# First stage of a streaming encoder on one core: small vectors by GpSimd's queue, the second tile's x loaded behind the second conditions, the first tile two quarters ahead, and throwaway products

## The chip, the core and the metric

The kernel runs on one core of one Trainium2 chip. A core has a matrix engine (TensorE, PE in the profile; PEld is its loading of the stationary operand), a vector engine (VectorE, DVE), an activation engine (ScalarE, ACT), GpSimd (POOL) and SyncE (SP), each with its own queue of instructions that it runs in order. DMA transfers are issued from the queues of SP, ACT or POOL (SPq, ACTq, POOLq) and run beside the engines. The metric is the device time of one execution in microseconds, the median of several runs.

## The reference

One inference step of a two-layer encoder on 1024 prompt rows and 32 sample rows of width 1024. The first layer's mixer, with which this case is concerned, is:

```python
mod = jax.nn.silu(c) @ w_ada[i] + b_ada[i]
sh1, sc1, gt1, sh2, sc2, gt2 = jnp.split(mod[:, None, :], N_MOD, axis=-1)
h = rmsnorm(x, g_norm[i, 0]) * (1 + sc1) + sh1
z = jax.nn.gelu(h @ w_in)
u, v = jnp.split(z, 2, axis=-1)
v = rmsnorm(v, g_v)
s = jnp.einsum('gij,bnjgd->bnigd', w, vr) + b_s      # per chunk of 128 rows
mix = (u * s) @ w_out
x = x + gt1 * rmsnorm(mix, g_norm[i, 1])
```

A channel MLP (1024 to 4096 to 1024, squared ReLU) follows; the second layer has a pooling mixer in place of the gating one. All is float32.

## The kernel before

The 1056 rows are three column tiles: 384, 384 and 256 + 32. x is kept transposed, features on partitions, as eight blocks of 128 (kb 0 to 7). Every weight is split into a high part `wh` (an activation copy rounded to the matrix engine's reduced float32, L422) and a low part `wl` (a subtraction on VectorE), every activation likewise into `hh` and `hl`, and a product is the sum of three: `wh*hh`, `wh*hl`, `wl*hh`.

All loads of x, conditioning weights (w_ada) and layer weights stand in one list, `stream`. `issue()` issues them in the list's order from SP (one load of x from ACT), as far as buffers are free: the first sixteen pieces of w_ada have buffers of their own, layer weights share three raw buffers. `stream_to(kind, key)` emits the work on the list up to a piece. Every hardware-issued DMA takes one of eight semaphores in turn and waits until the transfer that had it before has landed.

The first stage is written out by hand, in a block in which each engine keeps the order of the text (`tc.manual_schedule()`, from `load_vectors(2, slice(0, 2))` on). Its steps, by the names that the profile shows:

- `load_vectors`: the conditions c, then g_norm, b_ada, pool_scale and sgu_g_v, as rows (tile `row`). `turn_conditions`: silu, then a transpose (`csilT`). `turn_vectors`: transposes of the rows (`rowT`).
- `x_squares` (ACT, `xsq`): the sum of squares of a block of 128 rows of x. `x_turn`: eight PE transposes (`xT`), with two copies to `acc`, both on VectorE in tile 0, one on VectorE and one on ACT in tile 1.
- `first_norm(t)`, a generator for tile t, with the pieces `spread` (`ms_h`, `r_h`, then `pb_h` on PE and a copy by ACT), "statistics", and then `apply`: for two feature blocks at a time a scaling `mt` (VectorE), `hh` (ACT) and `hl` (VectorE). `h0`, `h1`, `h2` are the three generators, `next(h0)` emits the next piece.
- Conditioning: `do_ada_pe` multiplies silu(c) with two pieces of w_ada (`ada`, PE) and transposes the result on VectorE (`adas`). A fold, popped from `pe_folds` in the order made, gathers it on PE (`adat`) and writes scale coefficients (`coef`) or shifts (`shift`) on VectorE. `conditions(q)` does both groups (scale and shift) of quarter q, that is of feature blocks 2q and 2q + 1, and pops the first fold.
- `early_mm(bs, q)`: the first quarter-width piece of v (512 of its columns), for the row blocks bs and the feature quarter q: per block four products with `wh` (hh, hl by turns) and two with `wl`, all of 128x512 (`pv`, L973). Blocks 0 to 2 are tile 0 (called front below), 3 and 4 are tile 1 (rear); block 5 and tile 2 follow behind the stage. `early_ps` are the five PSUM banks in which they add up. Five blocks, four quarters and six products make the 120 early products.

The order of the text: conditions, x of blocks 0 and 1, vectors, x of block 2, conditions 0, statistics of tile 0; then for each quarter q: `apply` of tile 0, the products of blocks 0 to 2, (at q = 0 all of tile 1's x and statistics), `apply` of tile 1, conditions(q + 1) with a fold, the products of block 3, the other fold, the products of block 4.

What follows, from `stream_to("x", 8)` on, is tile 2's x, block 5's products and the rest of v; it is the same text in both kernels. Behind it a planner that counts PE and VectorE time weaves loading, conditioning and residual work between the products; its counts do not depend on the order inside the first stage. `sgu_group(g)` loads the spatial weights (`wt`, SP) and biases (`bs`, ACT) of a gating group, with two buffers each; the first two groups' loads have nothing to wait for and are issued during the first stage.

## Time and profile before

| | us |
|---|---|
| median of 3 runs | 2172.68 (2172.6 to 2174.59) |
| the profiled execution | 2173.74, span 2171.7 |
| PE busy | 2145.5 (99% of the span) |
| DVE, ACT, POOL busy | 1431.8, 971.3, 13.3 |
| first early product starts | 19.77 |
| x of tile 2 starts to be transposed | 68.20 |

How to read the profile: times count from the first instruction. A stretch row gives its bounds, its length, then for PE, PEld, DVE, ACT and POOL the busy time and the number of instructions, then the granted clock of TensorE (1.00 is full speed; before the first change that was recorded, at 15.89, the column shows 1.00 whatever it was), the busy share of the DMA engines and the GB/s moved. A timeline row gives start and duration, engine (with q: its queue issuing a DMA), line, operation, out<-in, shapes, the number of instructions merged, and in brackets the engine's idle time before it and what ended it. A row of the chain of waits is start, duration and what the chain ran through. Matmul ends are modelled: a matmul's row has a tail of about 0.39 us that overlaps the next.

### The profile page before, as it was taken

The numbers are of one execution on the slowest core, as the hardware profiler recorded it, in microseconds if no ns is written. First come the engines' busy times: TensorE is split into PE (matmuls) and PEld (weight loads), VectorE is DVE, ScalarE is ACT, GpSimd is POOL, SyncE is SP. The second block draws the span as 40 slices with busy tenths as digits, with TensorE's granted clock in tenths as the row PEclk, the third lists the DMA queues.
The fourth block names the chain that finished last, engine by engine and source line by source line (L and its number), as shares of the span: only waits on it lengthen the run. The fifth ranks groups of instructions, "written<-read, shape, count | busy, mean of one in ns | idle before, by whom it ended". The sixth has DMA issues, their size and how long they took to land.

```text
span 2171.7 us, 33210 instructions
## 1 busy us (share of the span) xinstructions
PE 2145.5 (99%) x13214; PEld 2078.1 (96%) x13214; DVE 1431.8 (66%) x2499; ACT 971.3 (45%) x1643; POOL 13.3 (1%) x30
## 2 busy tenths in 40 slices
PE   7999999999999999999999999999999999999998
PEld 5778899999999999999999999999999999999997
DVE  5688647566879548496747879869675554523377
ACT  4633422234447552323445566666555542313354
POOL 0000000000000000000000000000000000000001
PEclk9999999999999999999999999999999999999999
DMA  8386534343437454243645466565455552302255
GB/s 300 119 269 193 173 93 139 90 148 109 147 96 233 132 155 143 87 140 110 196 129 161 141 189 182 171 191 158 141 161 158 157 155 68 98 20 78 69 139 125
DMA packets 383262, 312.95 MB, mean 144 GB/s; under 512 B 39458, under 2 KB 346346, under 8 KB 383108
## 3 DMA queue, kind: packets, MB, share of 16 engines
q1 hardware_dynamic: 380452, 308.64, 46.8%
q8 instruction: 103, 1.69, 0.3%
q10 hardware_dynamic: 2144, 1.41, 0.2%
q0 software_dynamic: 512, 0.79, 0.1%
q14 instruction: 51, 0.42, 0.1%
HBM read 278.95 MB, written 31.84 MB: 143 GB/s over the span
## 4 chain that ended last, share of the span: by engine, by line
PE 93%; DVE 3%; DMA 2%; ACT 1%; issue 1%; ACTq 0%; DVEq 0%; SPq 0%
PE pg L902 11%; PE pg L903 11%; PE pg L904 11%; PE pf L902 11%; PE pf L904 11%; PE pf L903 11%; PE po L902 3%; PE po L903 3%; PE po L904 3%; PE pu L902 3%; PE pu L904 3%; PE pu L903 3%; PE pv L929 2%; PE pv L930 2%; PE pv L931 2%; PE pp L1532 1%
## 5 line engine op out<-in xcount | busy, mean ns | idle before, releaser
L902 PE MATMUL pg<-fh,wh_dn 128*128 128x384 f32 (+1 forms) x1536 | 495.8, 323 | 0.0
L902 PE MATMUL pf<-hh,wh_up 128*128 128x384 f32 (+1 forms) x1536 | 494.4, 322 | 0.0
L903 PE MATMUL pf<-hl,wh_up 128*128 128x384 f32 (+1 forms) x1536 | 493.1, 321 | 0.0
L904 PE MATMUL pf<-hh,wl_up 128*128 128x384 f32 (+1 forms) x1536 | 492.9, 321 | 0.2 <-DVE wl_up L79 0.2
L903 PE MATMUL pg<-fl,wh_dn 128*128 128x384 f32 (+1 forms) x1536 | 492.6, 321 | 0.4 <-DVE fl L79 0.4
L904 PE MATMUL pg<-fh,wl_dn 128*128 128x384 f32 (+1 forms) x1536 | 492.5, 321 | 0.0
L79 DVE TENSOR_TENSOR wl_up<-raw,wh_up 128x1024 fp32r<-128x1024 f32 x152 | 185.9, 1224 | 165.4 <-ACT wh_up L422 165.4
L902 PEld LDWEIGHTS pg<-fh,wh_dn 128*128 128x128 f32 x1536 | 288.3, 188 | 1.5 <-ACT fh L1121 0.6
L903 PEld LDWEIGHTS pg<-fl,wh_dn 128*128 128x128 f32 x1536 | 288.3, 188 | 1.5 <-DVE fl L79 0.7
L904 PEld LDWEIGHTS pf<-hh,wl_up 128*128 128x128 f32 x1536 | 288.6, 188 | 0.5 <-DVE wl_up L79 0.5
L903 PEld LDWEIGHTS pf<-hl,wh_up 128*128 128x128 f32 x1536 | 288.3, 188 | 0.4
L902 PEld LDWEIGHTS pf<-hh,wh_up 128*128 128x128 f32 x1536 | 288.2, 188 | 0.4
L904 PEld LDWEIGHTS pg<-fh,wl_dn 128*128 128x128 f32 x1536 | 288.3, 188 | 0.0
L422 ACT ACTIVATE wh_up<-raw 128x1024 fp32r<-128x1024 f32 x152 | 161.2, 1060 | 279.9 <-PE pf L903 213.6
L79 DVE TENSOR_TENSOR acc<-acc,pg 128x384 f32<-128x384 f32 (+1 forms) x336 | 174.2, 519 | 146.3 <-PE pg L904 145.7
L422 ACT ACTIVATE wh_dn<-raw 128x1024 fp32r<-128x1024 f32 x152 | 160.8, 1059 | 202.9 <-PE pg L903 170.6
L79 DVE TENSOR_TENSOR wl_dn<-raw,wh_dn 128x1024 fp32r<-128x1024 f32 x152 | 186.0, 1224 | 82.4 <-ACT wh_dn L422 82.2
L79 DVE SCALAR_TENSOR_TENSOR aa<-raw,csil,aa 128x512 f32<-128x512 f32 (+1 forms) x364 | 203.5, 623 | 8.0 <-DMA raw<-in_w_ada_dram 7.9
L1295 ACT ACTIVATE r<-pf 128x384 f32<-128x384 f32 (+1 forms) x192 | 86.6, 451 | 201.9 <-PE pf L904 199.2
L79 DVE TENSOR_TENSOR fl<-r,fh 128x384 fp32r<-128x384 f32 (+1 forms) x192 | 100.3, 523 | 85.4 <-ACT fh L1121 84.3
L902 PE MATMUL pu<-hh,wh_u 128*128 128x384 f32 (+1 forms) x384 | 125.8, 328 | 0.0
L902 PE MATMUL po<-ush,wh_o 128*128 128x384 f32 (+1 forms) x384 | 123.5, 322 | 0.0
(263 smaller groups left out, 2927.2 us busy)
## 6 DMA issues: line engine op xcount, KB each, us to landing
raw<-in_ffn_w_up_dram SPq DMA_DIRECT2D x152, 512.0 KB, 3.9
raw<-in_ffn_w_down_dram SPq DMA_DIRECT2D x152, 512.0 KB, 3.5
raw<-in_w_ada_dram SPq DMA_DIRECT2D x96, 512.0 KB, 4.3
raw<-in_sgu_w_in_dram SPq DMA_DIRECT2D x40, 512.0 KB, 4.4
xd<-acc SPq DMA_DIRECT2D x8, 1536.0 KB, 7.8
raw<-in_sgu_w_out_dram SPq DMA_DIRECT2D x24, 512.0 KB, 4.0
xo_r<-xd SPq DMA_DIRECT2D x32, 384.0 KB, 3.4
vd<-vt SPq DMA_DIRECT2D x32, 256.0 KB, 4.5
```

Of the source, the lines that this page charges most:

```text
L79: return op(out, *args, **kw)
L422: act(out=wh, in_=r, func=AF.Copy)
L902: mm(ps[:, :n], wh, rh, start=i == 0, stop=False)
L903: mm(ps[:, :n], wh, rl, start=False, stop=False)
L904: mm(ps[:, :n], wl, rh, start=False, stop=i == last)
L929: mm(ps[:m, :], a_h, wh[:, o : o + 512], start=k == 0, stop=False)
L930: mm(ps[:m, :], a_h, wl[:, o : o + 512], start=False, stop=False)
L931: mm(ps[:m, :], a_l, wh[:, o : o + 512], start=False, stop=k == KB - 1)
L1295: act(out=r[:, :n], in_=ps[:, :n], func=AF.Relu)
L1532: mm(ps[:, :n], wg[:, k, e * P : (e + 1) * P], A(t, 2 * g + k), start=k == 0, stop=k == 1)
```

## The change

- The four small vector loads (g_norm, b_ada, pool_scale, sgu_g_v) go by GpSimd's queue; only the conditions stay on ACT's. x of block 2 is loaded from SP.
- In the list of loads, x of tile 1 (blocks 3 to 5) stands behind the second conditions and the second quarter of v, not behind the first.
- `early_mm` takes one half of a quarter: with `wh`, or with `wl` (`second`); the `wl` subtraction of every quarter is emitted late, by `late_lo`.
- `warm(n)` multiplies a tile of ones with itself, 128x512, into the bank of block 4, which the first true product of that block clears: 10 such products at the start, 2 behind x of block 1, 6 ahead of the first quarter.
- x's squares of tile 1 are emitted beside its transposes (`x_sums`) and not when the load is reached.
- The stage's order: front quarters 0 and 1 (with tile 1's x between and behind), statistics of tile 1, rear quarters 0 and 1, then front and rear of quarters 2 and 3. Folds stand by themselves (`fold()`).
- The gating groups' `wt` and `bs` are both issued by SP, and not ahead of the load of v's piece 2, quarter 3, in the second stage.

```diff
@@ -177,10 +177,10 @@
     vec_rows = [t_m(f"row{i}") for i in range(3)]
-    def load_vectors(i, part):
+    def load_vectors(queue, i, part):
         at = sum(k for _, k in rows[i][: part.start])
         for ap, k in rows[i][part]:
-            nc.scalar.dma_start(vec_rows[i][at : at + k, :P], ap)
+            queue.dma_start(vec_rows[i][at : at + k, :P], ap)
             at += k
 
     csil = small.tile([P, KB, NV], F32, name="csil")
@@ -342,7 +342,7 @@
         for j in (8 + 2 * q, 9 + 2 * q, 2 * q, 2 * q + 1):
             add_ada(0, j)
         add_w(*v_item(0, q))
-        if q == 0:
+        if q == 1:
             for b in range(3, 6):
                 add_x(b)
     first_ada = len(stream)
@@ -407,7 +407,7 @@
                 r = work.tile([P, 1024], F32, tag="W", bufs=W_SLOTS, name=f"raw{k}")
             if kind == "x":
                 nr = P if key < 8 else DEC
-                i = (nc.scalar if key == 2 else nc.sync).dma_start(
+                i = nc.sync.dma_start(
                     r[:nr], ap.rearrange("t (k n) -> t k n", n=P)
                 )
             else:
@@ -421,7 +421,7 @@
         wl = work.tile([P, 1024], F32R, tag="W", bufs=W_SLOTS, name="wl_" + "_".join(map(str, key)))
         act(out=wh, in_=r, func=AF.Copy)
         witem[key] = (wh, wl)
-        if key == ("v", 0, 0):
+        if key[:2] == ("v", 0):
             late_lo.append(lambda: tt(out=wl, in0=r, in1=wh.bitcast(F32), op=ALU.subtract))
         else:
             tt(out=wl, in0=r, in1=wh.bitcast(F32), op=ALU.subtract)
@@ -589,13 +589,18 @@
 
 
     x_turns = deque()
+    x_sums = deque()
 
     def do_x(b, r):
-        x_squares(b, r)
         if b < 3:
+            x_squares(b, r)
             x_turn(b, r)
+            return
+        if b >= 6:
+            x_squares(b, r)
         else:
-            x_turns.append(lambda: x_turn(b, r))
+            x_sums.append(lambda: x_squares(b, r))
+        x_turns.append(lambda: x_turn(b, r))
 
     def stream_ready():
         k = state["next"]
@@ -958,25 +963,31 @@
     early_ps = [(ps_dn if b < 3 else ps_up)(f"pv0_{b}") for b in range(5)]
     h0, h1, h2 = (first_norm(t) for t in range(NT))
 
-    def early_mm(bs, q):
+    def early_mm(bs, q, second):
 
         wh, wl = witem[("v", 0, q)]
-        for second in (False, True):
-            for b in bs:
-                t, c0 = b // 3, b % 3 * P
-                tick(0.46 if second else 0.92)
-                for k in range(2):
-                    kb = 2 * q + k
-                    a_h, a_l = hh[t][:, kb, c0 : c0 + P], hl[t][:, kb, c0 : c0 + P]
-                    w = slice(k * 512, k * 512 + 512)
-                    for a in (a_h,) if second else (a_h, a_l):
-                        mm(
-                            early_ps[b],
-                            a,
-                            (wl if second else wh)[:, w],
-                            start=kb == 0 and a is a_h and not second,
-                            stop=kb == KB - 1 and second,
-                        )
+        for b in bs:
+            t, c0 = b // 3, b % 3 * P
+            tick(0.46 if second else 0.92)
+            for k in range(2):
+                kb = 2 * q + k
+                a_h, a_l = hh[t][:, kb, c0 : c0 + P], hl[t][:, kb, c0 : c0 + P]
+                w = slice(k * 512, k * 512 + 512)
+                for a in (a_h,) if second else (a_h, a_l):
+                    mm(
+                        early_ps[b],
+                        a,
+                        (wl if second else wh)[:, w],
+                        start=kb == 0 and a is a_h and not second,
+                        stop=kb == KB - 1 and second,
+                    )
+
+    fresh = onesr.unsqueeze(1).broadcast_to([P, 4, P])
+
+    def warm(n):
+
+        for _ in range(n):
+            mm(early_ps[4].rearrange("p (a b) -> p a b", a=4), onesr, fresh, start=True, stop=True)
 
     def early_end(bs):
         for b in bs:
@@ -986,47 +997,83 @@
 
         stream_to("ada", (0, 4 + q, 1))
         stream_to("ada", (0, q, 1))
+
+    def fold():
         pe_folds.pop(0)()
 
+    front, rear = (0, 1, 2), (3, 4)
+
+    def turn_x():
+        x_turns.popleft()()
+        x_sums.popleft()()
+
     with tc.manual_schedule():
-        load_vectors(2, slice(0, 2))
+        load_vectors(nc.scalar, 2, slice(0, 2))
         issue()
-        load_vectors(2, slice(2, 4))
-        load_vectors(0, slice(0, 1))
-        load_vectors(1, slice(0, 1))
+        load_vectors(nc.gpsimd, 0, slice(0, 1))
+        load_vectors(nc.gpsimd, 1, slice(0, 1))
+        load_vectors(nc.gpsimd, 2, slice(2, 4))
+        warm(10)
         turn_conditions()
         stream_to("x", 1)
+        warm(2)
+        stream_to("x", 2)
         turn_vectors()
-        stream_to("x", 2)
         next(h0)
-        conditions(0)
+        stream_to("ada", (0, 4, 1))
         statistics(h0)
+        stream_to("ada", (0, 0, 1))
+        fold()
         stream_to("w", ("v", 0, 0))
-        pe_folds.pop(0)()
-        for q in range(4):
-            next(h0)
-            if q == 0:
-                late_lo.pop()()
-            early_mm((0, 1, 2), q)
-            if q == 0:
-                stream_to("x", 5)
-                next(h1)
-                x_turns.popleft()()
-                x_turns.popleft()()
-                next(h1)
-                x_turns.popleft()()
-                statistics(h1)
-            next(h1)
-            if q < 3:
-                conditions(q + 1)
-                stream_to("w", ("v", 0, q + 1))
-                early_mm((3,), q)
-                pe_folds.pop(0)()
-                early_mm((4,), q)
-                if q == 2:
-                    stream_to("x", 6)
-            else:
-                early_mm((3, 4), q)
+        fold()
+        warm(6)
+        next(h0)
+        late_lo.pop()()
+        early_mm(front, 0, False)
+        early_mm(front, 0, True)
+        conditions(1)
+        fold()
+        stream_to("x", 5)
+        x_turns.popleft()()
+        fold()
+        next(h0)
+        x_sums.popleft()()
+        early_mm(front, 1, False)
+        late_lo.pop()()
+        turn_x()
+        early_mm(front, 1, True)
+        turn_x()
+        next(h1)
+        conditions(2)
+        statistics(h1)
+        fold()
+        next(h1)
+        early_mm(rear, 0, False)
+        early_mm(rear, 0, True)
+        fold()
+        next(h1)
+        early_mm(rear, 1, False)
+        early_mm(rear, 1, True)
+        stream_to("w", ("v", 0, 2))
+        next(h0)
+        early_mm(front, 2, False)
+        late_lo.pop()()
+        conditions(3)
+        early_mm(front, 2, True)
+        fold()
+        next(h1)
+        early_mm(rear, 2, False)
+        fold()
+        early_mm(rear, 2, True)
+        stream_to("w", ("v", 0, 3))
+        next(h0)
+        early_mm(front, 3, False)
+        late_lo.pop()()
+        next(h1)
+        stream_to("x", 6)
+        early_mm(rear, 3, False)
+        early_mm(front, 3, True)
+        early_mm(rear, 3, True)
         stream_to("x", 8)
         while x_turns:
             x_turns.popleft()()
@@ -1141,9 +1188,10 @@
 
     def sgu_group(g):
         wt = sgu.tile([P, P], F32, tag="wt", bufs=2, name=f"wt{g}")
-        nc.sync.dma_start(wt, sgu_w_s[0, g])
         bb = sgu.tile([P, P], F32, tag="bs", bufs=2, name=f"bs{g}")
-        nc.scalar.dma_start(bb, sgu_b_s[0, g].partition_broadcast(P))
+        with tc.issue_after(loads[("v", 2, 3)]):
+            nc.sync.dma_start(wt, sgu_w_s[0, g])
+            nc.sync.dma_start(bb, sgu_b_s[0, g].partition_broadcast(P))
 
         def turn():
             pt = ps_ms(f"wsT{g}")
```

## The prediction

> **What bounds the kernel now.** Read first: the page's busy times (of a span of 2171.7 us), then stretches of the span with the granted clock.
>
> ```profile
> PE 2145.5 (99%) x13214; PEld 2078.1 (96%) x13214; DVE 1431.8 (66%) x2499; ACT 971.3 (45%) x1643; POOL 13.3 (1%) x30
> ```
> ```profile
> 86.67:2171.00 2084.33, 2072.65 (x12753) 2024.88 (x12753) 1386.64 (x2379) 926.98 (x1563) 12.63 (x24) 1.00 0.47 141
> 19.77:68.36 48.59, 45.18 (x296) 32.19 (x297) 27.81 (x57) 21.12 (x38) 0.00 (x0) 0.90 0.64 222
> ```
>
> Columns: stretch, its length, busy time (count) of PE, PEld, DVE, ACT, POOL; clock, DMA share, GB/s. From 86.67 us on TensorE is the bound, at full clock, so whatever the first stage gains or loses reaches the end unchanged. The stage's mark is 68.36 us, the end of the last early product; behind it both kernels do the same in the same order, so I take the shift at 68.36 as the shift of the total. The profiled execution took 2173.74 us, 1.06 above the median of 2172.68; the sum is made against 2173.74.
>
> The stage itself is not bound by work. First, what starts it:
>
> ```profile
> 7.66 8.50 DMA raw<-in_w_ada_dram
> 19.77 0.79 PE pv L973
> ```
> ```profile
> 7.00:9.70 2.70, 2.70 (x14) 2.70 (x14) 1.83 (x7) 2.66 (x5) 0.00 (x0) 1.00 1.07 352
> 9.70:12.50 2.80, 2.66 (x12) 1.90 (x11) 1.82 (x5) 1.64 (x4) 0.00 (x0) 1.00 0.51 147
> 17.00:41.00 24.00, 19.10 (x123) 14.00 (x122) 13.09 (x30) 12.07 (x23) 0.00 (x0) 0.79 1.07 391
> ```
> ```profile
> 7.40 0.35 ACTq L1146 DMA_DIRECT2D bs<-in_sgu_b_s_dram  x1
> 6.60 0.26 PE L198 MATMUL csilT<-ident,row 16*128 16x16 f32 x1 [6.60 <-ACT row L194]
> ```
>
> The chain of waits says that the fourth conditioning piece lands at 16.16 (7.66 + 8.50), and that the first product starts 3.6 us later, at 19.77. Between 9.70 and 12.50 the transfers run at 147 instead of 391 GB/s: (391 - 147) x 2.8 = 0.68 MB, 1.75 us lost, behind a bs load on ACT's queue (7.40). TensorE's own first work waits until 6.60 for the conditions.
>
> Second, the clock, on stretches of equal length:
>
> ```profile
> 15.89:19.30 3.41, 1.93 (x34) 1.32 (x30) 1.82 (x6) 2.02 (x5) 0.00 (x0) 1.00 1.03 416
> 19.30:22.71 3.41, 2.94 (x6) 2.11 (x7) 2.44 (x4) 3.35 (x7) 0.00 (x0) 0.50 1.07 386
> 22.71:26.13 3.42, 3.42 (x9) 2.64 (x8) 0.83 (x5) 1.12 (x3) 0.00 (x0) 0.50 1.08 384
> 26.13:29.54 3.41, 2.99 (x21) 2.36 (x19) 1.38 (x2) 0.98 (x2) 0.00 (x0) 1.00 1.08 386
> 32.95:36.37 3.42, 1.70 (x37) 0.88 (x29) 3.01 (x7) 2.19 (x4) 0.00 (x0) 1.00 1.08 388
> 36.37:39.78 3.41, 3.41 (x16) 2.26 (x17) 1.93 (x5) 0.00 (x0) 0.00 (x0) 0.50 1.09 381
> ```
>
> The clock changes only on this grid. A stretch with 1.70 or 1.93 us busy is followed by half clock; a fully busy one lifts it again, one with 2.94 does not. The products in the half-speed stretches cost twice.
>
> Third, pieces of work and their waits, from the timeline (idle time and who ended it in brackets):
>
> ```profile
> 67.29 1.07 PE L973 MATMUL pv<-wl_v,hh 128*128 128x512 f32 x4
> 45.53 1.93 PE L477 MATMUL ada<-raw,csil 128*32 128x256 f32 x32
> 27.08 2.04 PE L580 MATMUL xT<-ident,x_rows 128*128 128x128 f32 x16
> 30.09 1.07 PE L732 MATMUL pb_h<-r_h,ones 128*128 128x128 f32 x6 [0.98 <-ACT r_h L730]
> 36.04 0.24 PE L459 MATMUL adat<-adas,squares 128*32 128x4 f32 x8 [1.73 <-DVE adas L489]
> ```
> ```profile
> 38.96 0.29 PE L459 MATMUL adat<-adas,squares 128*32 128x4 f32 x8
> 39.32 0.16 DVE L79 TENSOR_TENSOR shift<-adat,vec 128x4 f32<-128x4 f32 x1 [1.44 <-PE adat L459]
> 40.04 1.14 ACT L875 ACTIVATE hh<-mt,shift 128x384 fp32r<-128x384 f32 x2 [4.22 <-DVE mt L79]
> 50.06 1.15 ACT L875 ACTIVATE hh<-mt,shift 128x384 fp32r<-128x384 f32 x2 [5.56 <-DVE mt L79]
> 50.73 0.50 PE L973 MATMUL pv<-wh_v,hh 128*128 128x512 f32 x1
> 51.38 0.19 PEld L973 LDWEIGHTS pv<-wh_v,hl 128*128 128x128 f32 x1 [0.47 <-DVE hl L79]
> ```
>
> A product at full clock: (1.07 - 0.39 of tail) / 3 = 0.228 us. A fold runs adat (PE), shift (DVE), scaling (DVE), hh (ACT), product (PE): 38.96 to 40.04, then 50.73 - 50.06 = 0.67, together 1.75, of which 0.25 is adat. Unless products lie behind the fold, TensorE waits 1.5. Before, the two folds of a quarter stand around the products of block 3, with block 4's 6 x 0.228 = 1.4 us behind the second, and the wait is hidden.
>
> **The stage before, as a sum.** 120 products x 0.228 = 27.4; three conditioning groups at 1.75 (1.93 less some overlap of its tail) = 5.25; 24 transposes at (2.04 - 0.27) / 15 = 0.118, 2.8; pb_h 0.9; six folds 1.5: 37.8. The half-speed stretches hold some 22 products that cost 0.2 more: 4.4. The rest of 48.59 is waits and tail: 6.4.
>
> **The change part by part.**
> *Small vectors and loads.* Four vector loads leave ACT's queue for POOL's, x of block 2 goes to SP, wt and bs go behind a load of the second stage. ACT's table load is no longer behind them, so the conditions are ready up to 1.3 us sooner; TensorE is then at the throwaways until 5.7, so 0.9 of it counts, inside the next term. POOL is idle then; its one kind of transfer lands 3.0 us (median) from the issue and two are issued in 1.33, so four land by 1.3 + 2.7 + 3.0 = 7; they are wanted behind the copies of blocks 0 and 1, at 6.6 + 4 x 0.69 = 9.4: nothing, a microsecond or two if POOL's first transfer is slow. With the 147 GB/s hole gone, the fourth conditioning piece lands at 7.23 (x of block 2, row below) + 4 x 0.524 MB / 391 GB/s = 12.6, some 0.3 more for small packets: 12.9. If the hole stays, 16.2: these are the ends. I take 12.9, since what precedes the hole (the bs loads) is gone. With the same 3.6 us behind it the first product starts at 16.5 instead of 19.77. The transposes allow that if they run at full clock: the copies behind them stood 0.85 apart (0.69 of work, 0.16 of waiting for TensorE).
>
> ```profile
> 1.68 5.55 DMA x_rows<-in_x_prompt_dram
> out_dram<-turned POOLq DMA_DIRECT2D x16, 48.0 KB, 3.0
> 2119.23 1.33 POOL L1619 DMA_DIRECT2D out_dram<-turned  x2 [2.13 <-issue]
> 10.50 0.69 DVE L586 COPY acc<-xT 128x512 f32<-128x512 f32 x1 [0.16 <-PE xT L580]
> ```
>
> *Throwaway products.* Ten at half clock (eight in 3.42 us from 22.71, 0.43 each, 4.3) run from about 1.4 to 5.7, where TensorE waited until 6.60: free. Two more cost 0.5 to 0.9 beside DVE's copies: free. Six behind the second fold take 1.4 (full) or 2.6 us (half) inside the 1.75 of the fold's own chain: 0 to 0.9; I take 0. They may keep the clock up to the first product, so that the first 18 cost 4.1 instead of 7.4.
> *Three loads of x later, second conditions earlier.* At 391 GB/s a 512 KB load is 1.34 us: second conditions land by 19.3, v's second quarter at 20.7, x of block 5 at 24.7, all ahead of their use below: nothing.
> *The order of the products.* Work is the same 37.8. The waits are new, each by the rows above:
> front quarter 0: hl 0.4. Front quarter 1: the fold for shift stands last, 1.5 + hl 0.4. Rear quarter 0: block 5's square now runs behind its transposes; copy 0.6, square 1.25, statistics 1.75 (rows below, 23.63 to pb) make 3.6, less 1.93 of conditions: 1.7; then pb to product 0.03 + 0.53 + 0.66 + 0.67 = 1.9 less 0.25 of fold: 1.65, + 0.4. Rear quarter 1: the fold of quarter 2 stands ahead of the scaling on DVE, which needs nothing of it: 1.5 + 0.4. Rear quarter 2: the same, 1.5 + 0.4. Front quarter 3: 1.5 less four products, 0.6 + 0.4. Rear quarter 3: 0.3 + 0.4. With 0.5 of small ones: 12.0.
>
> ```profile
> 22.48 1.06 ACT L565 ACTIVATE xsq<-x_rows 128x1024 f32<-128x1024 f32 x1
> 23.66 0.17 DVE L79 TENSOR_SCALAR ms_h<-ssx 128x3 f32<-128x3 f32 x1 [1.62 <-ACT xsq L565]
> 24.71 0.16 DVE L79 SCALAR_TENSOR_TENSOR r_h<-q_h,r_h 128x3 f32<-128x3 f32 x1
> 29.65 0.97 ACT L730 ACTIVATE r_h<-ident,r_h 128x128 f32<-128x128 f32 x3
> 17.78 0.49 ACT L893 ACTIVATE r_h<-pb_h 128x384 f32<-128x384 f32 x1 [1.39 <-PE pb_h L732]
> 18.31 1.15 DVE L79 SCALAR_TENSOR_TENSOR mt<-acc,coef,r_h 128x384 f32<-128x384 f32 x2 [0.15 <-ACT r_h L893]
> ```
>
> At full clock the mark is 16.5 + 37.8 + 12.0 + 0.4 of tail = 66.7, 1.7 earlier than 68.36.
> *The clock under these waits.* The two waits at the statistics leave about 1 us of work in 4.4, less than the 1.70 of 3.42 after which the clock fell. The pairs 1.5 + 0.4 leave 1.3 to 1.7 when they fall inside one stretch. A fall costs at least one stretch, 8 products x 0.2 = 1.6 (36.37 to 39.78), and lasts as long as no stretch is full. Ends: none (0) and five (8). I take three (one surely at the statistics, two among the four pairs and for a stretch that does not fill): 4.8. Mark 71.5, shift +3.1.
> *wt and bs on SP.* bs no longer occupies ACT (0.33 us each, ACT is idle half the time): 0. SP waits for a buffer in its place; loads are three ahead: 0, at most a few us.
>
> **Sum:** 2173.74 - 3.3 (start) - 4.4 (old half speed) + 12.0 - 6.0 (new waits, old waits without the tail) + 4.8 (new half speed) = 2176.8, 4.2 above the median of the runs before.
>
> The Trainium skill, "TensorE: Matmul & The Clock Gate", Part 1, lets the clock fall only after a whole window of some 3.4 us without work and warns of gaps over about 3 us; by that, waits of 1.7 us would cost no clock (rival 1). The trace disagrees: 1.73 us of idle time, with 1.70 of 3.42 busy, were enough at 36.37. Its Part 4 says that transposes do not count as work, so the clock lifted by the throwaways would be lost at once (rival 2). Here 26.13 to 29.54, mostly transposes, kept 1.00.
>
> **The rivals.**
> 1. The clock stays up: half-idle stretches do not always lower it. The row below, 1.82 us busy, kept full clock. Then 2173.74 - 1.7 = 2172.0. Against: the two falls above.
>
> ```profile
> 84.16:87.57 3.41, 1.82 (x9) 1.19 (x8) 2.71 (x6) 2.03 (x5) 0.00 (x0) 1.00 0.72 244
> ```
>
> 2. The start isn't won: the hole stays (+3.3, 2180.1), or the throwaways don't hold the clock and the first conditions and 18 products run at half speed (some 1.5 + 3.3 more, 2181.6).
> 3. Faster: the new order's fold waits are hidden after all, because DVE's scaling runs ahead of the fold. 1.5 x 3 + 0.6 = 5.1 less, and with the clock up 2172.0 - 5.1 = 2166.9. It decides (under 2168.3) once 3.7 of the 5.1 are gone. Against: 39.32 shows DVE idle 1.44 behind a fold, in written order.
> 4. SP, waiting for bs's buffer, delays a weight load in the gating stage: 2 to 5 us, 2180. For it: bs's buffer came free 22 us after wt's.
>
> ```profile
> 298.32 0.35 SPq L1144 DMA_DIRECT2D wt<-in_sgu_w_s_dram  x1
> 320.85 0.33 ACTq L1146 DMA_DIRECT2D bs<-in_sgu_b_s_dram  x1
> ```
>
> **How the numbers follow.** Forecast 0.40 (2174.8 to 2179.8; 0.2% over 2172.68, about what a measurement of this kernel can tell from no change, is 2177.0, so 0.23 of it is slower and 0.17 the same); rival 1 0.15, the same; rival 2 0.27 and rival 4 0.07, slower; rival 3 0.11, faster. Slower 0.57, same 0.32, faster 0.11. The range 2171.5 to 2182 leaves out rival 3 and the worst of rival 2.
>
> **What would show it.** First product near 16.5 and no stretch near 150 GB/s by 13 us: the start. TensorE idle 1.5 behind adat ahead of four of the quarters, 1.7 ahead of pb_h: the waits. Clock 0.50 in some three stretches between 26 and 64 us: the falls. Last early product near 71.5. Wrong if the clock stays at 1.00 or the waits are under 1 us.

## The result, and the profile after

The changed kernel takes 2179.32 us in the median of 8 runs (2174.88 to 2182.26), the kernel before 2171.77 (2169.63 to 2174.59). The ratio is 1.0034, with a 95% interval of 1.0024 to 1.0044: the change makes the kernel slower by a third of a per cent. The forecast was 2176.8, range 2171.5 to 2182.0.

The profiled execution took 2179.16 us, 5.42 more than the profiled execution before. TensorE's busy time on the page is 6.1 us above that of before:

```profile
PE 2151.6 (99%) x13232; PEld 2081.2 (96%) x13232; DVE 1431.7 (66%) x2499; ACT 971.0 (45%) x1643; POOL 15.4 (1%) x34
```

Only 18 instructions were added, the throwaways, and most of them run where TensorE was idle. So the same products must be dearer. The stretches of the span say where:

```profile
93.26:2177.00 2083.74, 2072.87 (x12753) 2024.87 (x12753) 1386.98 (x2379) 926.32 (x1563) 12.49 (x24) 1.00 0.47 141
17.82:75.27 57.45, 48.55 (x296) 33.34 (x297) 27.81 (x57) 21.37 (x38) 0.00 (x0) 0.88 0.52 185
9.70:12.50 2.80, 2.08 (x22) 0.91 (x20) 2.38 (x11) 1.70 (x5) 0.00 (x0) 1.00 1.09 390
```
```profile
72.84 2.43 PE L977 MATMUL pv<-wl_v,hh 128*128 128x512 f32 x10
```

Behind 93 us the two kernels are alike (12753 instructions, 2072.87 against 2072.65 us busy). In these two executions the whole loss lies between the first early product (17.82) and the mark, the end of the last one (72.84 + 2.43 = 75.27): 57.45 us for 296 instructions that took 48.59 before. The start is better, but by less than forecast: the first product comes 1.95 us earlier. The stretch that moved 147 GB/s before now moves 390.

The timeline shows TensorE's waits in the stage. The four that end on hh were not there before; the one ahead of pb_h was 0.98 then, and the old wait of 1.73 ahead of adat is gone:

```profile
27.41 0.50 PE L977 MATMUL pv<-wh_v,hh 128*128 128x512 f32 x1 [1.46 <-ACT hh L880]
...
39.05 1.07 PE L737 MATMUL pb_h<-r_h,ones 128*128 128x128 f32 x6 [1.53 <-ACT r_h L735]
...
42.01 0.49 PE L977 MATMUL pv<-wh_v,hh 128*128 128x512 f32 x1 [1.70 <-ACT hh L880]
...
48.68 0.49 PE L977 MATMUL pv<-wh_v,hh 128*128 128x512 f32 x1 [1.46 <-ACT hh L880]
...
61.75 0.50 PE L977 MATMUL pv<-wh_v,hh 128*128 128x512 f32 x1 [1.66 <-ACT hh L880]
```

And the clock, on its own grid of 3.41 us:

```profile
25.66:29.08 3.42, 1.81 (x15) 1.08 (x14) 3.16 (x7) 2.78 (x5) 0.00 (x0) 1.00 1.09 382
29.08:32.49 3.41, 3.41 (x11) 2.51 (x10) 0.59 (x1) 0.00 (x0) 0.00 (x0) 0.50 1.07 393
...
35.90:39.32 3.42, 1.89 (x34) 0.98 (x26) 1.57 (x8) 2.35 (x7) 0.00 (x0) 1.00 1.06 410
39.32:42.73 3.41, 1.55 (x16) 1.03 (x15) 2.17 (x6) 1.90 (x4) 0.00 (x0) 1.00 0.96 282
42.73:46.14 3.41, 3.41 (x8) 2.73 (x9) 0.41 (x1) 0.00 (x0) 0.00 (x0) 0.50 0.04 16
46.14:49.56 3.42, 1.80 (x14) 0.95 (x13) 2.12 (x5) 1.55 (x3) 0.00 (x0) 1.00 0.00 0
49.56:52.97 3.41, 3.41 (x9) 2.59 (x9) 3.26 (x6) 1.68 (x3) 0.00 (x0) 0.50 0.00 0
...
59.80:63.21 3.41, 1.60 (x13) 0.92 (x13) 2.53 (x6) 2.09 (x3) 0.00 (x0) 1.00 0.01 2
63.21:66.62 3.41, 3.41 (x16) 2.27 (x16) 1.11 (x3) 0.39 (x1) 0.00 (x0) 0.50 0.00 0
```

Four stretches run at half clock, and each follows a stretch that holds one of the four waits for hh. The fifth wait, ahead of pb_h, lies in the stretch at 35.90, and full clock follows it. A kernel shown below (*the order mended*) does the same 296 instructions wholly at full clock with 41.52 us busy; that gives the price of the half clock in both kernels, and the stage in three terms. Another (*bs late*) does them at full clock in the order of before with 41.07, so the terms of the work and of the half clock are good to about half a microsecond:

| | before | after | difference |
|---|---|---|---|
| first early product | 19.77 | 17.82 | -1.95 |
| the work at full clock | 41.5 | 41.5 | 0 |
| idle time of TensorE (length less busy time) | 3.4 | 8.9 | +5.5 |
| half clock (busy time less 41.5) | 3.7 | 7.0 | +3.3 |
| mark | 68.36 | 75.27 | +6.9 |

From the mark to the end of the span it is 2177.3 - 75.27 = 2102.0 us, against 2171.7 - 68.36 = 2103.4 before: 1.35 us come back behind the stage, and 5.6 of the 6.9 reach the end of the span. By the medians the change costs 7.55 us: the profiled execution before was 1.97 above the median of its kernel, the one after 0.16 below.

### The profile page after: what moved, and what is told of

The parts are those of the page before. It is cut to its first block, busy times and chain, and to the rows that moved or that the text cites. A ratio compares the mean times of both kernels' runs of the same rounds, so it can differ in the third digit from the quotient of the medians.

```text
span 2177.3 us, 33255 instructions
## 1 busy us (share of the span) xinstructions
PE 2151.6 (99%) x13232; PEld 2081.2 (96%) x13232; DVE 1431.7 (66%) x2499; ACT 971.0 (45%) x1643; POOL 15.4 (1%) x34
## 3 DMA queue, kind: packets, MB, share of 16 engines
q8 instruction: 103, 1.69, 0.3%
## 4 chain that ended last, share of the span: by engine, by line
PE 93%; DVE 3%; DMA 2%; ACT 1%; issue 1%; DVEq 0%; ACTq 0%; SPq 0%
PE pf L907 11%; PE pg L907 11%; PE pf L909 11%; PE pg L909 11%; PE pf L908 11%; PE pg L908 11%; PE po L908 3%; PE po L907 3%; PE po L909 3%; PE pu L907 2%; PE pu L909 2%; PE pu L908 2%; PE pv L935 2%; PE pv L934 2%; PE pv L936 2%; PE pv L977 1%
```

## The experiments

Twelve kernels, in three groups; each group was compared with runs of the kernel before on the same chip, so the ratios compare better than the medians. "First" and "mark" are those of the profiled execution. "Half" counts the half-speed stretches between its first early product and its mark. A profiled execution is one of a spread of several us: that of *loads alone* is 1.7 under the median of its kernel, that of *squares early* 5.7 above. So marks compare less well than ratios.

| kernel | median us | ratio to before, 95% interval | first | mark | half |
|---|---|---|---|---|---|
| before | 2171.45 to 2172.33 in the groups | 1 | 19.77 | 68.36 | 3 |
| changed | 2179.32 | 1.0034 [1.0024, 1.0044] | 17.82 | 75.27 | 4 |
| no throwaways | 2182.34 | 1.0043 [1.0029, 1.0057] | 19.42 | 77.69 | 5 |
| start alone | 2168.01 | 0.9987 [0.9979, 0.9996] | 17.97 | 63.60 | 1 |
| folds moved | 2171.08 | 1.0001 [0.9992, 1.0010] | 20.16 | 68.99 | 2 |
| waits filled | 2176.99 | 1.0029 [1.0017, 1.0041] | 19.72 | 71.63 | 0 |
| loads alone | 2170.96 | 0.9997 [0.9988, 1.0006] | 19.01 | 65.37 | 1 |
| throwaways alone | 2171.49 | 0.9998 [0.9989, 1.0007] | 20.69 | 65.11 | 0 |
| start, waits filled | 2168.03 | 0.9983 [0.9974, 0.9991] | 19.67 | 65.01 | 0 |
| order mended | 2167.45 | 0.9979 [0.9971, 0.9988] | 18.00 | 61.74 | 0 |
| order mended, 13 at the head | 2169.28 | 0.9986 [0.9977, 0.9994] | 19.97 | 63.44 | 0 |
| squares early | 2177.77 | 1.0026 [1.0017, 1.0035] | 18.26 | 74.36 | 4 |
| changed, 13 at the head | 2178.74 | 1.0029 [1.0019, 1.0038] | 18.26 | 75.74 | 4 |
| bs late | 2170.48 | 0.9989 [0.9980, 0.9998] | 19.10 | 63.84 | 0 |

The theory to be tested was the prediction's: the new order puts five waits of about 1.5 us into the stage, each wait brings down the clock, and the start wins only a part of it back. Its rivals: it is the start that fails (loads or throwaways), or the clock alone and not the waits.

### No throwaways

```
-        warm(10)
         turn_conditions()
         stream_to("x", 1)
-        warm(2)
 ...
         fold()
-        warm(6)
```

> The changed kernel without its 18 throwaway products. Theory (the loss is the new waits of the written order and the falls of the clock behind them; the throwaways pay): the first conditions and most of the first 18 products run at clock 0.50, 3 to 5 us slower than the changed kernel's 2179.3, so 2182 to 2184. Rival (the throwaways stand in the path and are the loss): 3 us or more faster, under 2176.5.

Measured 2182.34 us, ratio 1.0043, 3.0 us above the changed kernel; the intervals of the two overlap, so the size is known only roughly. The profiled execution shows what the throwaways do. Stretches of it:

```profile
17.32:20.73 3.41, 1.40 (x12) 0.80 (x13) 2.90 (x9) 1.15 (x2) 0.00 (x0) 1.00 1.08 406
...
19.42:77.69 58.27, 49.56 (x296) 33.84 (x297) 27.82 (x57) 21.38 (x38) 0.00 (x0) 0.85 0.48 170
```

Without the six products ahead of the first early one the stretch holds only 1.40 us of work, and the clock falls just as the early products begin; the clock first rose at 10.49. So the throwaways are not the cause of the loss; by the medians they pay, and the overlap leaves open how much.

### The start alone

The order of the products, the x list and the conditions stay as in the kernel before; only the start is that of the change:

```
-        load_vectors(2, slice(2, 4))
-        load_vectors(0, slice(0, 1))
-        load_vectors(1, slice(0, 1))
+        load_vectors(nc.gpsimd, 0, slice(0, 1))
+        load_vectors(nc.gpsimd, 1, slice(0, 1))
+        load_vectors(nc.gpsimd, 2, slice(2, 4))
+        warm(10)
 ...
+        warm(2)
 ...
+        warm(6)
         for q in range(4):
 ...
-        nc.sync.dma_start(wt, sgu_w_s[0, g])
+        with tc.issue_after(loads[("v", 2, 3)]):
+            nc.sync.dma_start(wt, sgu_w_s[0, g])
+            nc.sync.dma_start(bb, sgu_b_s[0, g].partition_broadcast(P))
```

> The kernel before with the change's start alone: vectors by GpSimd's queue, x of block 2 by SP, wt and bs late, throwaways, the start's order up to the first quarter; the order behind it and the place of tile 1's x as before. Theory: first product near 17.8 instead of 19.77 and the first 18 products at full clock, 2 + 3 us, so 2166 to 2169, faster than before. Rival (the loads or the throwaways cost): 2172 or more.

Measured 2168.01 us, ratio 0.9987 (0.9979 to 0.9996): faster than both kernels. Its stretches:

```profile
29.90:33.31 3.41, 1.69 (x18) 1.24 (x14) 3.14 (x7) 1.56 (x3) 0.00 (x0) 1.00 1.08 390
33.31:36.72 3.41, 3.41 (x16) 2.66 (x16) 2.92 (x7) 1.15 (x2) 0.00 (x0) 0.50 1.09 389
17.97:63.60 45.63, 42.12 (x296) 30.45 (x297) 27.81 (x57) 21.16 (x38) 0.00 (x0) 0.96 0.65 227
```

With the same first product as in the changed kernel (17.97 against 17.82), the stage takes 45.63 us instead of 57.45, in the order of before. That is the plainest reading of the study: what the change does behind the start (the new order, with x of tile 1 and its squares later and every `wl` late) costs 11.8 us in this stage and 11.3 at the end (2179.32 - 2168.01), and the start is a gain. The one half-speed stretch left follows the wait of 1.72 that was there before.

### The folds moved

Three folds of the changed kernel no longer stand directly ahead of the products that need them:

```
         early_mm(rear, 0, True)
-        fold()
         next(h1)
+        fold()
         early_mm(rear, 1, False)
 ...
         late_lo.pop()()
+        next(h1)
         conditions(3)
         early_mm(front, 2, True)
         fold()
-        next(h1)
-        early_mm(rear, 2, False)
         fold()
+        early_mm(rear, 2, False)
         early_mm(rear, 2, True)
```

> The changed kernel with three folds moved so that VectorE's scalings that need nothing of them, or work of TensorE, stand around them: rear quarters 1 and 2 and front quarter 3. Theory: the waits of 1.46 and 1.66 ahead of rear quarters 1 and 2 go, 0.5 to 1 at front quarter 3, and one or two of the half-speed stretches behind them, so 3.5 to 7 us less: 2172.5 to 2176. Rival (the wait only moves to the next step): 2178 or more.

Measured 2171.08 us, ratio 1.0001 (0.9992 to 1.0010): 8.2 us less than the changed kernel, better than the 2172.5 to 2176 expected. Its timeline has three of the five waits left:

```profile
29.77 0.49 PE L977 MATMUL pv<-wh_v,hh 128*128 128x512 f32 x1 [1.46 <-ACT hh L880]
...
41.41 1.07 PE L737 MATMUL pb_h<-r_h,ones 128*128 128x128 f32 x6 [1.53 <-ACT r_h L735]
...
44.37 0.50 PE L977 MATMUL pv<-wh_v,hh 128*128 128x512 f32 x1 [1.71 <-ACT hh L880]
```
```profile
20.16:68.99 48.83, 43.67 (x296) 31.47 (x297) 27.78 (x57) 21.37 (x38) 0.00 (x0) 0.93 0.56 198
```

The waits of 1.46 and 1.66 at the rear's quarters 1 and 2 are gone, and two half-speed stretches with them. Of the 57.45 - 48.83 = 8.6 us that the stage loses, 3.7 are idle time (8.90 to 5.16) and 4.9 busy time (48.55 to 43.67): the clock was worth more than the waits. No work was taken away; a few instructions moved in the written order.

### The waits filled

Six throwaways stand in each of the five waits of the changed kernel (into a spare PSUM tile where the block's own is in use). One of the five:

```
         next(h0)
         x_sums.popleft()()
+        warm(6)
         early_mm(front, 1, False)
```

> The changed kernel with six throwaway products (1.4 us) in each of five waits: ahead of front quarter 1, of tile 1's statistics, and of rear quarters 0, 1 and 2. The waits stay. Theory (the falls of the clock come from the waits and cost about 1.6 each): no stretch at 0.50 behind the first quarter, 4 to 6 us less, 2173 to 2175. Rival (the clock does not follow the waits, or the throwaways delay what waits): 2178 or more.

Measured 2176.99 us, ratio 1.0029: 2.3 us less than the changed kernel, inside the intervals, and above the 2173 to 2175 expected. In the profiled execution the clock stays at 1.00 through the whole stage, though nothing useful is done in the waits. Stretches and timeline:

```profile
19.72:71.63 51.91, 50.32 (x326) 34.12 (x327) 27.81 (x57) 21.38 (x38) 0.00 (x0) 1.00 0.53 189
1072.17:1075.59 3.42, 1.58 (x8) 1.00 (x6) 1.30 (x2) 2.39 (x3) 0.00 (x0) 1.00 0.60 198
1075.59:1079.00 3.41, 2.96 (x9) 2.97 (x10) 3.41 (x5) 2.54 (x5) 0.00 (x0) 0.50 0.61 174
```
```profile
1074.72 0.44 PE L907 MATMUL pg<-fh,wh_dn 128*128 128x384 f32 x1 [1.42 <-ACT fh L1174]
1076.04 0.69 PE L908 MATMUL pg<-fl,wh_dn 128*128 128x384 f32 x1 [0.87 <-DVE fl L79]
```

The stage takes 51.91 us instead of 57.45, so the clock alone is worth 5.5 us there; this shows that the idle time of the waits brings it down, since only idle time was replaced. But 4.3 of these us are lost far behind the stage in this execution (2177.9 - 71.63 = 2106.3 us against 2102.0): at 1073 and 1075 us TensorE waits for ACT and DVE 1.42 and 0.87 us, and the clock falls there. Why those waits are longer here than in the changed kernel (0.28 at the same place) wasn't tried. So the gain at the end is smaller than in the stage, and only the gain in the stage is shown.

### The loads alone, and the throwaways alone

Two halves of the start on the order of before. The first is the start alone without its three `warm` lines; the second adds only these to the kernel before:

```
         issue()
         load_vectors(2, slice(2, 4))
         load_vectors(0, slice(0, 1))
         load_vectors(1, slice(0, 1))
+        warm(10)
         turn_conditions()
         stream_to("x", 1)
+        warm(2)
 ...
+        warm(6)
         for q in range(4):
```

> The kernel before with the loads of the change only (small vectors by POOL, x of block 2 by SP, wt and bs late, the start's order), no throwaway products. If the loads make most of what the whole start gained (3.4 us of 2171.5), this gives 2168 to 2169.5. If the throwaways make most of it, the first product comes some 2 us sooner but TensorE idles at the head, the clock falls before the first products, and the first 18 products cost 7 us instead of 4: 2170.5 to 2172.5. I expect the second.

> The kernel before with the 10, 2 and 6 throwaway products only; loads and order as before. If the throwaways make most of the start's gain: the stretch ahead of the first product is full, the half clock at 19.3 to 26.1 of the trace before is gone, 2168 to 2170, with the first product still at 19 to 20 us. If the loads make most of it: 2170.5 to 2172, no better than before.

Measured 2170.96 us (ratio 0.9997) and 2171.49 us (0.9998): neither differs measurably from before, while the whole start gives 0.9987. The intervals are too wide to say that the whole is more than the sum of the halves. The second contradicts the forecast made for it (2168 to 2170). Its profile, stretches and timeline, shows why:

```profile
9.70:12.50 2.80, 2.34 (x26) 1.41 (x25) 2.11 (x7) 1.89 (x5) 0.00 (x0) 1.00 0.67 193
```
```profile
14.54 0.64 PE L477 MATMUL ada<-raw,csil 128*32 128x256 f32 x8 [2.26 <-DMA raw<-in_w_ada_dram]
16.04 0.64 PE L477 MATMUL ada<-raw,csil 128*32 128x256 f32 x8 [0.86 <-DMA raw<-in_w_ada_dram]
...
20.69 0.39 PE L973 MATMUL pv<-wh_v,hh 128*128 128x512 f32 x1
```

With the loads as before, TensorE gets to the conditioning pieces sooner and waits 3.1 us for the last two; the transfers still stand at 193 GB/s between 9.70 and 12.50. The clock falls in that wait (half from 16.70 to 20.11, ahead of the first product) and the first product is later than before. Read so, each half would remove one of two chains that are nearly equally long: the loads, and the half-speed work ahead of the first product. The next experiment does not fit this reading.

### bs late

Of the loads, only wt and bs are moved:

```
-        nc.sync.dma_start(wt, sgu_w_s[0, g])
         bb = sgu.tile([P, P], F32, tag="bs", bufs=2, name=f"bs{g}")
-        nc.scalar.dma_start(bb, sgu_b_s[0, g].partition_broadcast(P))
+        with tc.issue_after(loads[("v", 2, 3)]):
+            nc.sync.dma_start(wt, sgu_w_s[0, g])
+            nc.sync.dma_start(bb, sgu_b_s[0, g].partition_broadcast(P))
```

> The kernel before with wt and bs loaded behind the load of the second stage, and nothing else. The loads alone (with POOL and SP) gave 2170.96, first product 19.01. If the stretch at 147 GB/s came from the bs loads: it is gone, the fourth conditioning piece lands near 13 instead of 16.16, and the total is that of the loads alone, 2170 to 2171.3. If it came from the small vectors on ACT's queue or from x of block 2 there: the stretch stays, the piece lands near 16, and the time is that of before, 2171.3 to 2172.2.

Measured 2170.48 us, ratio 0.9989 (0.9980 to 0.9998). The stretch that stood at 147 GB/s:

```profile
9.70:12.50 2.80, 2.66 (x12) 1.90 (x11) 1.78 (x5) 1.60 (x4) 0.00 (x0) 1.00 1.07 378
```

The small vectors and x of block 2 are still on ACT's queue, and the hole is gone. Of the two loads moved, wt was issued only at 34.02 us in the kernel before, so the hole came from the early bs loads (7.40 and 9.05). The other moves of loads show no gain of their own (0.9997 with them, 0.9989 without, overlapping).

By itself this edit gives as much as the whole start (0.9989 against 0.9987): by the medians nothing shows that the throwaways add to it. In the profiled execution the clock also stays at 1.00 through the stage without a throwaway, although the wait ahead of adat (1.73, ending at 32.78) is as long as in the kernel before. It begins in this stretch and ends in the next:

```profile
28.86:32.27 3.41, 1.93 (x32) 0.94 (x32) 2.50 (x6) 2.72 (x5) 0.00 (x0) 1.00 1.08 394
```

In the kernel before the same wait lay whole within one stretch (32.95 to 36.37, 1.70 busy), and half clock followed. So what a wait costs also depends on where the clock's grid cuts it, and that differs from execution to execution.

### The start alone, its waits filled

Four throwaways ahead of the second tile's pb_h and seven ahead of its adat:

```
                 x_turns.popleft()()
+                warm(4)
                 statistics(h1)
 ...
         stream_to("ada", (0, q, 1))
+        if q == 1:
+            warm(7)
         pe_folds.pop(0)()
```

> The whole start on the order of before, plus 4 throwaways ahead of pb_h (wait 0.98) and 7 ahead of adat (wait 1.72) of the second tile. If the two waits cost a clock stretch: full clock through the whole first stage, mark 63.6 to 62, total 2166 to 2167.5. If the clock of one stretch is worth nothing at the end, because the time comes back in a wait far behind (as in the kernel with five waits filled, near 1075 us), 2167.5 to 2169.

Measured 2168.03 us against 2168.01 without them. The clock stays at 1.00 from 10.78 to the end of the work, yet first product to mark takes 45.34 us, only 0.3 less than 45.63: the seven fill the wait of 1.72, but the four came to stand behind pb_h, where the wait was only 0.35. Filling the waits of this order brings nothing that can be measured; what its one half-speed stretch costs was not measured apart.

### The order mended

The changed kernel with the folds moved, and four more things: the squares of blocks 3 to 5 as their x lands, the second tile's statistics and first scaling ahead of the third conditions, block 4's transposes between the scaling of the front's second quarter and its products, and one fold between the halves of rear quarter 0. A part of the edit:

```
         fold()
         next(h0)
-        x_sums.popleft()()
+        x_turns.popleft()()
         early_mm(front, 1, False)
         late_lo.pop()()
-        turn_x()
+        x_turns.popleft()()
+        next(h1)
         early_mm(front, 1, True)
-        turn_x()
-        next(h1)
-        conditions(2)
         statistics(h1)
-        fold()
         next(h1)
+        conditions(2)
         early_mm(rear, 0, False)
+        fold()
         early_mm(rear, 0, True)
```

> The changed kernel with the folds moved and, besides, the squares of blocks 3 to 5 taken when their x lands, the second tile's statistics and first scaling ahead of the third conditions, and the front's second quarter scaled ahead of block 4's transposes. My theory (waits in the order, and the clock falls they bring, are the loss): the three waits left with the folds moved (1.46, 1.53, 1.71) go, with them one or two half-speed stretches: mark 62 to 65, total 2163 to 2167. Rival (the early products cannot pay, since what the stage gains beyond the start alone is taken back by loads or waits behind it): 2167.5 to 2170, no better than the start alone.

Measured 2167.45 us, ratio 0.9979 (0.9971 to 0.9988): faster than the kernel before and than the changed one. The median lies between the theory's range and the rival's; the mark, 61.74, is a little better than the theory's. Stretches and timeline:

```profile
18.00:61.74 43.74, 41.52 (x296) 28.95 (x297) 27.56 (x57) 21.25 (x38) 0.00 (x0) 1.00 0.67 240
```
```profile
27.89 0.50 PE L973 MATMUL pv<-wh_v,hh 128*128 128x512 f32 x1 [0.59 <-ACT hh L876]
...
34.30 1.07 PE L733 MATMUL pb_h<-r_h,ones 128*128 128x128 f32 x6 [0.64 <-ACT r_h L731]
...
41.71 0.50 PE L973 MATMUL pv<-wh_v,hh 128*128 128x512 f32 x1 [0.35 <-ACT hh L876]
```

The three waits fell from 1.46, 1.53 and 1.71 to 0.59, 0.64 and 0.35, and the clock no longer falls in the stage. This kernel keeps the start, the list of loads, the late `wl` and the products of two quarters ahead, so these are not what made the changed kernel slow; the places of its folds, transposes and statistics are. But against the start alone (0.9987) the intervals overlap: that the new order, mended, beats the old one isn't shown.

### Squares early

Of these edits only the first, on the changed kernel:

```
     def do_x(b, r):
+        x_squares(b, r)
         if b < 3:
-            x_squares(b, r)
 ...
-        if b >= 6:
-            x_squares(b, r)
-        else:
-            x_sums.append(lambda: x_squares(b, r))
         x_turns.append(lambda: x_turn(b, r))
```

> The changed kernel with one edit: the squares of blocks 3 to 5 are taken when their x lands, not behind each block's transposes. Theory (the statistics' chain of copy and square made the wait of 1.53 ahead of pb_h): that wait goes to under 0.3; with it 1.5 us and perhaps one of the four half-speed stretches: 2175 to 2178. Rival (ACT has no room there, and the squares delay the scaling of the front's second quarter instead): the wait of 1.46 grows by what the other loses, 2179 to 2181.

Measured 2177.77 us, ratio 1.0026, 1.5 less than the changed kernel, inside the intervals. Its timeline:

```profile
28.31 0.62 PE L973 MATMUL pv<-wh_v,hh 128*128 128x512 f32 x1 [1.89 <-ACT hh L876]
...
38.27 1.07 PE L733 MATMUL pb_h<-r_h,ones 128*128 128x128 f32 x6
```

The wait of 1.53 ahead of pb_h is gone, so the chain of copy and square made it. The rival is right in part: the front's wait grew from 1.46 to 1.89. Still four stretches run at half clock, since the wait behind pb_h (1.70) remains.

### Thirteen throwaways at the head

`warm(10)` becomes `warm(13)`, once on the mended order and once on the changed kernel. The reason: the same start had its first product at 17.8 to 18.3 in some profiled executions and at 19.7 to 20.2 in others.

> The mended order with 13 throwaways at the head instead of 10. In the profiled executions the clock rose at 4.9 to 6.5 us in some (first product at 17.8 to 18.0) and at 10.6 to 10.8 in others (first product at 19.7 to 20.2, the first 16 transposes 3.51 instead of 2.09 us). Theory: the ten, some 4.3 us, fill a whole stretch of the 3.41 us grid only when it begins at the right moment; thirteen, to about 6.9, join the transposes, so that it rises by 8 in every execution: first product 17.9 to 18.6, median 2166 to 2167, and a narrower spread than 2165.7 to 2169.3. Rival (the moment of the rise doesn't set the start; the copies behind the transposes do): 2167.2 to 2168.2, as with ten or a little more, because the conditions' transpose is 0.4 us later.

> The changed kernel with 13 throwaways at the head instead of 10. If the early rise of the clock carries to the end: executions in which it rose late gain up to 2 us, median 2177.5 to 2178.7 with the slowest executions (2180.9 to 2182.3) gone. If what the start wins is lost to where the later waits fall on the clock's grid: 2178.7 to 2180, spread as before.

Measured 2169.28 us (ratio 0.9986, with ten 0.9979) and 2178.74 us (1.0029, with ten 1.0034): no gain, the first above both of its forecasts, and the spread (2166.9 to 2172.3; 2174.9 to 2183.6) isn't narrower. The profiled execution of the first refutes half of the theory. Its stretches:

```profile
7.42:10.83 3.41, 3.41 (x28) 2.96 (x27) 3.21 (x9) 3.34 (x7) 0.00 (x0) 1.00 1.09 384
10.83:14.24 3.41, 2.02 (x22) 1.02 (x21) 2.58 (x11) 1.38 (x6) 0.00 (x0) 1.00 1.07 394
14.24:17.66 3.42, 3.21 (x30) 1.98 (x29) 0.20 (x1) 1.73 (x4) 0.00 (x0) 0.50 1.09 385
```

The clock did rise by 8 us, as expected, but it fell again at 14.24, behind the small waits for the vectors and for pb_h, and the first product came at 19.97. An early rise must also be held.

## Why the prediction came out as it did

The sign and the mechanism came out: waits of the predicted places and sizes, and a clock that falls on them. The time lies near the forecast (2179.32, forecast 2176.8) partly by luck, as two steps of the sum were off in the same direction. The mark was to move by +3.1 and moved by +6.9: the start fell short by 1.3, the idle time grew 0.5 less than forecast, and the half clock cost 2.9 more. What hid this is that 1.35 came back behind the stage, and that the sum was made against an execution of 2173.74 us, 1.97 above the median of the runs that were compared; between the medians the change costs 7.55 us, more than twice the +3.1.

**The start: forecast 16.5, measured 17.82.** The hole went, as forecast, *bs late* shows that it was the bs loads, and the fourth conditioning piece landed at 12.9, as forecast. The step that failed is "With the same 3.6 us behind it": the conditioning pieces are no longer what is late. The chain of waits to the first product:

```profile
1.35 3.29 DMA row<-in_c_sample_dram
...
6.46 0.20 PE csilT L198
...
7.28 3.69 DVE acc L586 x6
...
13.16 1.07 PE pb_h L737 x6
...
17.15 0.62 ACT hh L880
```

It holds no load after the conditions' own, which lands at 4.64. Behind it come DVE's copies of the first tile, the statistics, pb_h and the fold. The conditions' transpose starts at 6.46, not at 5.7: the vectors that went to POOL weren't what it waited for (it started at 6.60 with them on ACT's queue). It waits for the conditions to land and for ACT's table load (1.28) and silu behind them. POOL's vectors cost nothing, as said.

**The throwaways** are free at the head and keep the clock up to 29.08 in the profiled execution; without them it fell as the products began. That step holds for this kernel, though *bs late* kept the clock up without any, and except that the clock's first rise, and with it some 1.5 us of the start, is a matter of the execution (last section): rival 2 in part.

**The waits.** TensorE's waits in the stage after, in us, times and longest:

```profile
PE pv L977 <- ACT hh L880: 6.3, 4, 1.7
PE pb_h L737 <- ACT r_h L735: 1.5, 1, 1.5
PE pv L977 <- DVE hl L79: 0.8, 5, 0.2
```

No load is among them, so the later x and the earlier conditions cost TensorE no wait here, as forecast. Five waits of the forecast are there: 1.5, 1.7, 1.65, 1.5 and 1.5 were forecast, 1.46, 1.53, 1.70, 1.46 and 1.66 measured. The waits forecast for front quarter 3 (0.6) and rear quarter 3 (0.3) are not there. In whole, work and waits at full clock were to take 37.8 + 12.0 + 0.4 = 50.2 us from first product to mark; measured are 57.45 less 7.0 of half clock, 50.4. "The fold of quarter 2 stands ahead of the scaling on DVE, which needs nothing of it" was exact: moving that fold behind the scaling took the wait away.

**The clock** is the term that was mis-sized: three stretches at 1.6 were taken, four at 1.75 were measured (7.0 us in all). One had been put down to the statistics and two to the four pairs of a fold's wait and a wait for hl; all four pairs brought it down (front quarter 1, rear quarters 0, 1 and 2), and the wait of 1.53 ahead of pb_h, by itself, did not (the row at 35.90). Rival 1, that the clock stays up, is refuted for the changed kernel by its own rows, and by the kernel with the waits filled, which had no half-speed stretch in the stage. Rival 3, hidden fold waits, is refuted by the timeline.

**wt and bs on SP.** Rival 4 did not occur: the time from mark to end is 1.35 us shorter, not longer. "Whatever the first stage gains or loses reaches the end unchanged" holds only to such a microsecond here, and to four in the execution with the waits filled, where later waits were longer and the clock fell in them; why they were is open.

The Trainium skill, "TensorE: Matmul & The Clock Gate", Part 1, gives an idle window of about 3.4 us as the condition of a fall. The rows at 25.66, 39.32, 46.14 and 59.80 disagree: none has more than 1.86 us idle. The same part says that the window runs freely, so that the first rise shifts from run to run; there the traces agree (4.64 to 6.00 in some executions of one start, 10.63 to 10.78 in others).

## What to carry to other kernels

Before moving work ahead in a written order, write down for each product the chain that it needs (here transpose, fold, scaling, copy) and see which other products lie behind that chain; an order with the same work lost 11 us, with five chains that stood bare. A wait of TensorE of 1.5 us should be priced with the clock stretch that it can cost, which here was more than the wait itself. And test the parts of a bundle apart: here one part of the start, the later bs loads, gave as much as the whole.

## What the runs showed of the hardware

**The clock's first rise is a matter of the execution.** One start, ten throwaways of some 4.3 us: the rise came at 4.64 to 6.00 us or at 10.63 to 10.78. Timelines of the changed kernel and of the one with folds moved show the first 16 transposes:

```profile
6.59 2.09 PE L580 MATMUL xT<-ident,x_rows 128*128 128x128 f32 x16
```
```profile
7.56 3.51 PE L580 MATMUL xT<-ident,x_rows 128*128 128x128 f32 x16
```

Their first products start at 17.82 and 20.16. The times of the rise are those at which the traces' records of the clock begin; the clock column doesn't tell this, as it reads 1.00 ahead of them as well, but the durations do. Of the 2.34 us between the two first products the transposes account for 1.42; some 0.9 is another matter, as the conditions landed at 5.55 in the second execution and at 4.64 in the first. In the kernel with the waits filled, with a late rise too, the same transposes took 3.67. A single profiled execution therefore says less about a start than its medians do.

**Transposes alone lift the clock.** In the kernel with the folds moved it rose at 10.77. The stretch ahead of that holds the conditions' transpose and those of x, and nothing else of TensorE's:

```profile
7.36:10.77 3.41, 3.40 (x16) 3.37 (x17) 2.24 (x7) 3.37 (x5) 0.00 (x0) 1.00 1.09 384
```

**Neither a fall nor a rise has a sharp limit in TensorE's busy time.** Stretches with 1.40, 1.55, 1.60, 1.69, 1.80 and 1.81 us busy were followed by half clock, but so was one with 2.02 (22 instructions, at 10.83 with thirteen at the head), while 1.89 (34 instructions, at 35.90 in the changed kernel) was not; 1.93 was followed by it in the kernel before (at 15.89) and not in *bs late* (at 28.86). Of the half-speed stretches, 2.94 busy (before, at 19.30) and 3.03 (no throwaways, at 44.62) did not lift the clock, but 2.90 did (no throwaways, at 48.04): the prediction's "one with 2.94 does not" is no rule. What else is counted stays open.
